# Products of the second expert table 512 columns wide, and a recurrent mixer worked in two halves

## Chip, core and metric

The kernel runs on one core of one Trainium2 chip. The metric is the device time of one execution in microseconds; the time before is the median of three runs. Engines are named as the profile names them: PE is TensorE's matmul, PEld its weight load, DVE is VectorE, ACT is ScalarE, POOL is GpSimd, and SP issues the transfers.

## What is computed

Two blocks of layers run over 256 tokens of width 1024. In the first block each of two layers has a mixer and an expert feed-forward network; the layers' modulation vectors come from `cond @ w_ada`. The change touches the feed-forward network's second table, in both layers, and the second layer's mixer.

```python
def peer_ffn(h, w_q, sub_keys, u_tab, v_tab):
    ...                                   # ids, gate: 16 experts of 16384 for each head and token
    def block(args):
        hx, idx, g = args
        u = u_tab[idx]
        act = jax.nn.gelu(jnp.einsum('thkd,td->thk', u, hx).astype(jnp.float32))
        return jnp.einsum('thk,thkd->td', g * act, v_tab[idx])

def rglru_mixer(h, w_in, conv_w, conv_b, w_a, b_a, w_x, b_x, lam, w_out):
    xb, yb = jnp.split(h @ w_in, 2, axis=-1)
    y_gate = jax.nn.gelu(yb)
    xc = sum(xp[:, j:j + S] * conv_w[j] for j in range(CONV_W)) + conv_b
    def direction(d, reverse):
        r = jax.nn.sigmoid(block_diag_linear(xc, w_a[d], b_a[d]))
        ig = jax.nn.sigmoid(block_diag_linear(xc, w_x[d], b_x[d]))
        log_a = -LRU_C * r * jax.nn.softplus(-lam[d])
        a = jnp.exp(log_a)
        mult = jnp.sqrt(-jnp.expm1(2.0 * log_a))
        return lax.associative_scan(lin_combine, (a, mult * ig * xc), axis=1, reverse=reverse)[1]
    return ((direction(0, False) + direction(1, True)) * y_gate) @ w_out
```

## The kernel before

Activations lie feature-major: 128 features on the partitions, the 256 tokens along a row, eight such tiles for the width of 1024. Every float32 operand of a large product is split in two, a rounded high part (a cast on ACT, line 283) and the low rest (a subtraction on DVE or POOL, line 285), and `mm3` (lines 412 to 418) makes one 128x128 weight tile into three matmuls: high by high, high by low, low by high. `Stream` cuts a matrix into blocks of 1024 columns (512 KB, eight weight tiles); `prefetch` takes a block from HBM into one of the four `raw` buffers and splits it into one of three `whi`/`wlo` pairs.

The expert network does not gather. `peer` multiplies all 16384 experts: 128 chunks of the first table (U), then 128 chunks of the second (V), 128 experts each. In the V part the weights of a matmul are a 128x128 tile of the table and its moving operand is the 128x256 tile of gated activations `A`; `product` runs `mm3` for the chunk's eight tiles, so a chunk is 24 matmuls of 256 columns. The outputs accumulate over all chunks, feature-major, in four PSUM banks. The last three chunks are done output by output, with `residual` behind each pair, and `lead.products` starts the next layer's first weights before the norm is known.

In layer 0 the V part also carries the next layer's modulation: `ada_sums` takes 48 blocks of `w_ada` through the same `raw` buffers, adds each into a row on DVE (lines 711 and 713), and after each eight sums over the partitions with four narrow matmuls (line 717).

`lru` is the mixer. The input branch (`lru_xb`: four outputs by `lead`, four by `linear`) goes through the convolution `evac` into `XC`; the gates (`lru_bd`) follow, 16 outputs of two kinds, with a step on DVE for each and a product on POOL; then the output gate (`lru_yb`, eight outputs in all four PSUM banks of `mm`), woven with `recurrences`, which goes by steps over both halves: all exponentials, all square roots, then four scans. The split of the product and `lru_out` come at the end.

A scheduler orders the instructions of each engine by a timeline of its own; `behind` and `pin` add an order written by hand. So the program's order and the engines' order can differ.

## Time and profile before

| | |
|---|---|
| median of three runs (lowest, highest) | 3035.58 us (3031.94, 3043.15) |
| profiled execution: its time | 3039.8 us |
| its span, first to last instruction | 3038.0 us |
| mean granted TensorE clock | 0.977 |
| V part of layer 0 | 759.9 to 1144.5 us of the span |
| mixer of layer 1, to the last matmul of `lead.products` | 1159.65 to 1303.4 us |
| V part of layer 1 | 1775.2 to 2147.0 us |

A matmul's end is modelled in this profile, and the records of consecutive matmuls overlap. How fast TensorE goes is therefore read from the distance between two starts, and not from the duration of one.

### The profile page before, as it was taken

To read this page: it belongs to the slowest core of one execution; us is meant where nothing else is said; L and a number is where in the kernel's file an instruction comes from. 1 tells how busy PE (TensorE), PEld (TensorE's weight loads), DVE (VectorE), ACT (ScalarE), POOL (GpSimd) and SP (SyncE) were. 2 spreads that over 40 slices of the span, in tenths; PEclk is the share of its full clock that TensorE was granted. 3 is DMA by queue.
4 is the path that set the end of the run, shared out by engine and by line. 5 is a ranking of instruction groups with operands and counts; after the bars stand their busy time and mean duration, and the time that the engine had idled before them with its cause. 6 is when DMAs were issued, how large, how long until landed. Compare 5 with 4: busy or idle time off the path is not lost. (4 is left out here: it accounts for less than half of the span.)

```text
span 3038.0 us, 58214 instructions
## 1 busy us (share of the span) xinstructions
PE 2868.7 (94%) x23408; PEld 2768.7 (91%) x23408; DVE 2249.4 (74%) x4115; ACT 1480.1 (49%) x2584; POOL 416.1 (14%) x260
## 2 busy tenths in 40 slices
PE   7999989999999998798999999999999989999898
PEld 7988989999999997698999999999888889977898
DVE  8997996887567659899788855555754688665885
ACT  3335434444444445554444444444744666455663
POOL 2232231000000004513200000000132020211201
PEclk9999999999999999899999999999999999999999
DMA  7655445555678763454555555665444346543454
GB/s 254 202 186 164 143 144 175 156 161 168 205 258 272 253 215 113 124 170 145 161 158 160 161 171 182 183 185 182 152 81 73 109 141 184 178 121 83 145 181 132
DMA packets 140143, 503.66 MB, mean 166 GB/s; under 512 B 15816, under 2 KB 18776, under 8 KB 139488
## 3 DMA queue, kind: packets, MB, share of 16 engines
q1 hardware_dynamic: 139872, 499.93, 53.7%
q8 instruction: 184, 3.01, 0.4%
q14 instruction: 87, 0.71, 0.1%
HBM read 496.72 MB, written 1.05 MB: 164 GB/s over the span
## 5 line engine op out<-in xcount | busy, mean ns | idle before, releaser
L415 PE MATMUL psmm<-xh,whi 128*128 128x256 f32 x5488 | 1568.2, 288 | 45.0 <-ACT xh L463 18.3
L417 PE MATMUL psmm<-xh,wlo 128*128 128x256 f32 x5488 | 1560.5, 286 | 40.4 <-DVE wlo L285 36.2
L416 PE MATMUL psmm<-xl,whi 128*128 128x256 f32 x5488 | 1565.7, 286 | 5.3 <-DVE xl L554 2.8
L283 ACT CAST whi<-raw 128x1024 fp32r<-128x1024 f32 x819 | 857.5, 1048 | 1231.6 <-PE psmm L416 924.7
L285 DVE TENSOR_TENSOR wlo<-raw,whi 128x1024 fp32r<-128x1024 f32 x740 | 939.7, 1272 | 452.0 <-ACT whi L283 445.7
L415 PEld LDWEIGHTS psmm<-xh,whi 128*128 128x128 f32 x5488 | 1058.6, 194 | 57.8 <-ACT xh L463 19.8
L417 PEld LDWEIGHTS psmm<-xh,wlo 128*128 128x128 f32 x5488 | 1062.2, 194 | 46.9 <-DVE wlo L285 41.8
L416 PEld LDWEIGHTS psmm<-xl,whi 128*128 128x128 f32 x5488 | 1065.0, 194 | 9.6 <-DVE xl L554 4.8
L285 POOL TENSOR_TENSOR wlo<-raw,whi 128x1024 fp32r<-128x1024 f32 x90 | 229.3, 2552 | 492.9 <-ACT whi L283 429.7
L285 POOL TENSOR_TENSOR Ar<-raw,Ar 128x1024 fp32r<-128x1024 f32 x4 | 9.6, 2402 | 1310.4 <-ACT Ar L283 1310.4
L415 PE MATMUL psst<-xh,whi 128*128 128x256 f32 x400 | 119.8, 301 | 0.0
L416 PE MATMUL psst<-xl,whi 128*128 128x256 f32 x400 | 118.9, 298 | 0.3 <-DVE xl L645 0.3
L417 PE MATMUL psst<-xh,wlo 128*128 128x256 f32 x400 | 118.0, 296 | 0.7 <-DVE wlo L285 0.7
L415 PE MATMUL psmm<-yh,whi 128*128 128x256 f32 x352 | 98.2, 280 | 0.0
L417 PE MATMUL psmm<-yh,wlo 128*128 128x256 f32 x352 | 97.9, 278 | 0.0
L416 PE MATMUL psmm<-yl,whi 128*128 128x256 f32 x352 | 97.5, 277 | 0.0
L713 DVE SCALAR_TENSOR_TENSOR oh<-raw,cond,oh 128x1024 f32<-128x1024 f32 x42 | 53.9, 1284 | 55.8 <-DMA raw<-in_ada 55.8
L1198 DVE TENSOR_TENSOR oh<-io,sel 128x512 f16<-128x512 f16 x128 | 54.2, 424 | 52.8 <-PE psac L1210 26.9
L464 DVE TENSOR_TENSOR xl<-A,xh 128x512 fp32r<-128x512 f32 x128 | 87.1, 684 | 0.0
L416 PEld LDWEIGHTS psst<-xl,whi 128*128 128x128 f32 x400 | 79.1, 198 | 7.2 <-issue 5.2
L415 PEld LDWEIGHTS psst<-xh,whi 128*128 128x128 f32 x400 | 79.0, 198 | 5.5 <-issue 4.5
L417 PEld LDWEIGHTS psst<-xh,wlo 128*128 128x128 f32 x400 | 79.2, 198 | 4.3 <-issue 2.8
(576 smaller groups left out, 3924.2 us busy)
## 6 DMA issues: line engine op xcount, KB each, us to landing
raw<-in_U SPq DMA_DIRECT2D x256, 512.0 KB, 3.6
raw<-in_V SPq DMA_DIRECT2D x256, 512.0 KB, 3.7
raw<-in_up SPq DMA_DIRECT2D x88, 512.0 KB, 3.7
raw<-in_ada SPq DMA_DIRECT2D x80, 512.0 KB, 4.4
raw<-in_down SPq DMA_DIRECT2D x44, 512.0 KB, 3.7
raw<-in_ev_in SPq DMA_DIRECT2D x42, 512.0 KB, 3.6
raw<-in_hg_in SPq DMA_DIRECT2D x40, 512.0 KB, 3.7
raw<-in_peer_q SPq DMA_DIRECT2D x32, 512.0 KB, 3.9
```

Of the source, the lines that this page charges most:

```text
L283: keep(nc.scalar.copy(hi, raw))
L285: keep(eng.tensor_tensor(lo, raw, hi.bitcast(F32), op=OP.subtract))
L415: first = t.matmul(ps, w[0], x[0], start=start, stop=False, **kw)
L416: t.matmul(ps, w[0], x[1], start=False, stop=False, **kw)
L417: t.matmul(ps, w[1], x[0], start=False, stop=stop, **kw)
L464: s.nc.vector.tensor_tensor(lo, src, hi.bitcast(F32), op=OP.subtract)
L713: nc.vector.scalar_tensor_tensor(acc, raw, s.cond[:, k:k + 1], acc, op0=OP.mult, op1=OP.add)
L1198: nc.vector.tensor_tensor(o1l, io4, k1, op=OP.is_equal)
```

## The change

**V part.** The operands change places. The 128x128 weights of a matmul are now a token half of a chunk's activations, and the table's rows are the moving operand, 512 columns in one matmul. A chunk is 12 matmuls (two halves of the features, two halves of the tokens, three products) into four whole PSUM banks, token-major. After the last chunk the four banks are copied to SBUF (`tok`), 16 transposes of 128x128 turn them feature-major in the two `ac` banks (`features`), and `residual` reads from there.

**Modulation.** `ada_sums` takes its blocks into four slots of `A`, the rows of the first 16 chunks, once these are used (`room`), and no longer into the `raw` buffers.

**Mixer.** The four input outputs that `lead` doesn't cover are computed tile by tile of the input in four banks; the evacuation of `lead`'s outputs is done in place in PSUM and put behind the norm. Four outputs of the gate branch come before the gates. Steps that went over one output go over four (`R_` by its constant, the tanh). POOL's products go to DVE, and most splits go from POOL to DVE with the casts on ACT. `recurrences` is called for one half at a time: the first runs beside the second half's gates, the second beside the last gate outputs and the first half of `lru_out`, which now accumulates tile by tile of its input.

The core of the diff:

```diff
-        u = s.ker.splp.tile([128, S], F32, name="sq", tag="sq", bufs=SQB)
+
+        u = ps[:, 0:S] if s.name == "lru_xb" else s.ker.splp.tile([128, S], F32, name="sq", tag="sq", bufs=SQB)
         w = s.ker.leadw[:, j, :]
         if s.n > S:
             nc.vector.tensor_copy(w, ps[:, S:S + 2])
         if m is None:
-            nc.vector.tensor_tensor(u, ps[:, 0:S], r, op=OP.mult)
+            ins = nc.vector.tensor_tensor(u, ps[:, 0:S], r, op=OP.mult)
+            if s.name == "lru_xb":
+                s.ker.behind(ins, s.ker.last_norm)
...
-                raw = s.raw_block(s.d[f"ada{layer}"][((r - 1 + layer) * KD + k) * 2 + e])
+                ap = s.d[f"ada{layer}"][((r - 1 + layer) * KD + k) * 2 + e]
+                if room:
+                    raw = room[k % len(room)]
+                    nc.sync.dma_start(raw, ap)
+                else:
+                    raw = s.raw_block(ap)
...
-            s.linear(s.stream("lru_xb"), x, KD, KD, evac, spare=XB_SP)
-            bd = s.stream("lru_bd", lo_pool=lambda b: b % BD_LO, hi_dve=lambda b: b % 4 < BD_HI)
+
+            w = s.stream("lru_xb")
+            ld, s.lead = s.lead, None
+            others = [bank()[:, :S] for bank in (s.mm, s.mm, s.stat, s.stat)]
+            for k in range(KD):
+                for ps in others:
+                    s.mm3(ps, next(w), (x[0][:, k, :], x[1][:, k, :]), k == 0, k == KD - 1)
+            for o in range(LEAD):
+                evac(o, ld.output(o, s.r, s.m))
+            for o, ps in enumerate(others):
+                evac(LEAD + o, ps)
+            yb = s.stream("lru_yb")
+            bd = s.stream("lru_bd", lo_pool=lambda b: b > 4 and b % 2)
...
-                            nc.scalar.activation(dst[:, o, :], ps, AF.Sigmoid, bias=s.v(b, d * KD + o))
-                        w = R_[d][:, o, :]
-                        nc.vector.tensor_scalar(w, w, cc[:, d * KD + o:d * KD + o + 1], None, op0=OP.mult)
-                    sl = slice(2 * n, 2 * n + 2)
-                    nc.gpsimd.tensor_tensor(IG[d][:, sl, :], IG[d][:, sl, :], XC[:, sl, :], op=OP.mult)
-                if n % 2:
-                    for d in range(2):
-                        hv = halves[n // 2]
-                        order.append(nc.scalar.activation(TH[d][:, hv, :], R_[d][:, hv, :], AF.Tanh, scale=0.5))
...
-            def recurrences():
-                for hv in halves:
-                    for d in range(2):
-                        a, ig = R_[d][:, hv, :], IG[d][:, hv, :]
-                        queue(nc.scalar.activation(a, a, AF.Exp, scale=-1.0))
-                        nc.vector.scalar_tensor_tensor(ig, a, 1.0, ig, op0=OP.add, op1=OP.mult)
...
-                for hv in halves:
-                    for d in range(2):
-                        a, ig, th, hs = (T[d][:, hv, :] for T in (R_, IG, TH, HS))
...
-                    nc.vector.tensor_tensor(HS[0][:, hv, :], HS[0][:, hv, :], HS[1][:, hv, :], op=OP.add)
+
+            hi, lo = s.acts()
...
+            def recurrences(h, gelus):
+
+                hv = slice(4 * h, 4 * h + 4)
+                for d in range(2):
+                    r = R_[d][:, hv, :]
+                    c = s.lru_cc[:, d * KD + 4 * h:d * KD + 4 * h + 4, None].to_broadcast([128, 4, S])
+                    nc.vector.tensor_tensor(r, r, c, op=OP.mult)
+                    queue(nc.scalar.activation(TH[d][:, hv, :], r, AF.Tanh, scale=0.5))
+                    queue(nc.scalar.activation(r, r, AF.Exp, scale=-1.0))
+                    nc.vector.tensor_tensor(IG[d][:, hv, :], IG[d][:, hv, :], XC[:, hv, :], op=OP.mult)
+                yield
+                for d in range(2):
+                    queue(nc.scalar.activation(TH[d][:, hv, :], TH[d][:, hv, :], AF.Sqrt))
+                    nc.vector.scalar_tensor_tensor(IG[d][:, hv, :], R_[d][:, hv, :], 1.0, IG[d][:, hv, :],
+                                                   op0=OP.add, op1=OP.mult)
+                yield
+                for first in gelus:
+                    gelu(first)
+                for d in range(2):
+                    a, ig, th, hs = (T[d][:, hv, :] for T in (R_, IG, TH, HS))
+                    nc.vector.tensor_tensor(ig, ig, th, op=OP.mult)
...
-            gate = gate_branch()
-            run_all(islice(gate, YL))
-            weave(gate, recurrences())
...
+                for j in (2 * h, 2 * h + 1):
+                    sl = slice(2 * j, 2 * j + 2)
+                    t = HS[0][:, sl, :]
+                    nc.vector.tensor_tensor(t, t, HS[1][:, sl, :], op=OP.add)
+                    nc.vector.tensor_tensor(t, t, YG[:, sl, :], op=OP.mult)
+                    s.split_into(hi[:, sl, :], lo[:, sl, :], t)
+                    yield
+
+            run_all(gate_branch((0, 1), s.ac), gate_branch((2, 3), s.ac))
+            for first in (0, 2):
+                gelu(first)
+            run_all(gates(0), gates(1))
+            weave(chain(gate_branch((4, 5), s.stat), gates(2), gates(3)), recurrences(0, ()))
...
+            pss = []
+
+            def product(k, o):
+                s.mm3(pss[o // 2][:, o % 2, :], next(out), (hi[:, k, :], lo[:, k, :]), k == 0 and o % 2 == 0,
+                      k == KD - 1, skip_group_check=True)
+
+            def first_half():
+                pss.extend(s.mm().rearrange("p (a b) -> p a b", a=2) for _ in range(4))
+                for k in range(4):
+                    for o in range(KD):
+                        product(k, o)
+                    yield
+
+            weave(chain(gate_branch((6, 7), s.ac), first_half()), recurrences(1, (4, 6)))
+            ev = s.residual(1, 0, lead)
+            for k in range(4, KD):
+                for o in range(4):
...
+                    for k in range(4, KD):
+                        product(k, o + e)
+                for f in after:
+                    f()
+                after = [ev(o + e, pss[o // 2][:, e, :]) for e in range(2)]
...
-            acc = [s.mm().rearrange("p (a b) -> p a b", a=2) for _ in range(4)]
-            vt = s.stream(f"V{layer}")
+
+            acc = [[s.mm() for _ in range(2)] for _ in range(2)]
+            vt = s.stream(f"V{layer}", width=WBLK)
...
+                return next(vt), (wh[:, c % 8, :], wl[:, c % 8, :])
+
+            def product(c, half, tt, v, w):
+
+                ts, fs = slice(tt * 128, (tt + 1) * 128), slice(half * 512, (half + 1) * 512)
+                for i, (a, b) in enumerate(((0, 0), (0, 1), (1, 0))):
+                    nc.tensor.matmul(acc[half][tt], w[a][:, ts], v[b][:, fs], start=c == 0 and i == 0,
+                                     stop=c == NK - 1 and i == 2)
...
+                room = [Af[:, n * WBLK:(n + 1) * WBLK] for n in range(RAW_A)]
+                row = oh.rearrange("p a b c -> p (a b c)").bitcast(F32)[:, 0:WBLK]
+                extra = chain(*(s.ada_sums(1, r, row, room) for r in range(3)))
...
-                if c % 2 and c > 8:
+                for half in range(2):
+                    for tt in range(2):
+                        product(c, half, tt, v, w)
+                if c % 2 and c >= 4 * RAW_A:
                     next(extra, None)
...
+            def features(half, tok):
+
+                for j in range(2):
+                    pt = s.ac().rearrange("p (a b) -> p a b", a=2)
+                    for e in range(2):
+                        for tt in range(2):
+                            nc.tensor.transpose(pt[:, e, tt * 128:(tt + 1) * 128],
+                                                tok[:, tt, (2 * j + e) * 128:(2 * j + e + 1) * 128], s.ident)
+                    yield [ev(4 * half + 2 * j + e, pt[:, e, :]) for e in range(2)]
+
+            toks = []
+            for half in range(2):
+                tok = s.rawp.tile([128, WBLK], F32, name="tok", tag="raw").rearrange("p (a b) -> p a b", a=2)
+                for tt in range(2):
+                    for c, v, w in last:
+                        product(c, half, tt, v, w)
+                    (nc.vector.tensor_copy if tt else nc.scalar.copy)(tok[:, tt, :], acc[half][tt])
+                toks.append(tok)
...
-            for j in range(KD // 2):
-                for o in (2 * j, 2 * j + 1):
-                    for c, v, w in last:
-                        product(c, o, v, w)
-                for f in after:
-                    f()
-                after = [ev(o, acc[j][:, o % 2, :]) for o in (2 * j, 2 * j + 1)]
+            for half, tok in enumerate(toks):
+                for fs in features(half, tok):
+                    for f in after:
+                        f()
+                    after = fs
```

On PE, at the end of layer 0's V part, before (`whi`, `wlo`: the split table; `xh`, `xl`: the split activations; `Ar`: the next layer's lead input; the numbers tell buffers apart):

```order
L415 MATMUL psmm_9028<-xh_9023,whi_13104 128x256
L416 MATMUL psmm_9028<-xl_9024,whi_13104 128x256
L417 MATMUL psmm_9028<-xh_9023,wlo_13105 128x256
L415 MATMUL psac_13253<-Ar_13109 128x258
L415 MATMUL psac_13254<-Ar_13109 128x258
L415 MATMUL psmm_13255<-Ar_13109 128x258
```

The same place now (`tok`: the copied banks; `cst`: the identity):

```order
L1325 MATMUL psmm_9027<-wlo_11557,xh_9023 128x512
L1325 MATMUL psmm_9027<-whi_11556,xl_9024 128x512
L1325 MATMUL psmm_9028<-wlo_11557,xh_9023 128x512
L1325 MATMUL psmm_9028<-whi_11556,xl_9024 128x512
L1361 MATMUL psac_11628<-cst_80,tok_11586 128x128
L1361 MATMUL psac_11643<-cst_80,tok_11586 128x128
L1361 MATMUL psac_11628<-cst_80,tok_11586 128x128 x3
L1361 MATMUL psac_11643<-cst_80,tok_11586 128x128 x3
L1361 MATMUL psac_11660<-cst_80,tok_11607 128x128 x4
L420 MATMUL psmm_11697<-Ar_11561 128x258
L420 MATMUL psmm_11698<-Ar_11561 128x258
L1361 MATMUL psac_11677<-cst_80,tok_11607 128x128 x4
```

A matmul of twice the width stands for two, and 16 transposes stand between the last product and nearly all of the next layer's first products. The scheduler works all four banks to the end together, where the program finishes one half first.

On DVE, in the middle of layer 0's V part, before (`oh` holds the modulation's row, `cond` its factor; one `wlo` is one chunk of the table):

```order
L713 SCALAR_TENSOR_TENSOR oh_3392<-raw_10650,cond_90,oh_3392 128x1024
L464 TENSOR_TENSOR xl_9024<-A_2917,xh_9023 128x512
L285 TENSOR_TENSOR wlo_10623<-raw_10620,whi_10622 128x1024
L285 TENSOR_TENSOR wlo_10658<-raw_10655,whi_10657 128x1024
L713 SCALAR_TENSOR_TENSOR oh_3392<-raw_10715,cond_90,oh_3392 128x1024
```

The same place now:

```order
L725 SCALAR_TENSOR_TENSOR oh_3392<-A_2917,cond_90,oh_3392 128x1024
L469 TENSOR_TENSOR xl_9024<-A_2917,xh_9023 128x512
L535 SCALAR_TENSOR_TENSOR gsc_88<-mod1_86,vecs_76 128x8
L287 TENSOR_TENSOR wlo_9579<-raw_9576,whi_9578 128x1024
L725 SCALAR_TENSOR_TENSOR oh_3392<-A_2917,cond_90,oh_3392 128x1024
L287 TENSOR_TENSOR wlo_9597<-raw_9594,whi_9596 128x1024
```

The sums stood one to two chunks; now they stand nearly one to one. Counted over the whole part, all 48 lie within 51 chunks, where before they were spread over 99.

On DVE, around the scans of the mixer, before (`HS` are the scans' outputs, `TH` the square roots, `R` and `IG` the gates, `YG` the gate branch):

```order
L1057 SCALAR_TENSOR_TENSOR HS0_13395<-R0_13397,IG0_13399 128x1024
L1054 TENSOR_TENSOR IG1_13400<-IG1_13400,TH1_13402 128x1024
L1060 SCALAR_TENSOR_TENSOR HS1_13396<-R1_13398,IG1_13400 128x1024
L1057 SCALAR_TENSOR_TENSOR HS0_13395<-R0_13397,IG0_13399 128x1024
L1060 SCALAR_TENSOR_TENSOR HS1_13396<-R1_13398,IG1_13400 128x1024
L1063 TENSOR_TENSOR HS0_13395<-HS0_13395,HS1_13396 128x1024 x2
L1073 TENSOR_TENSOR HS0_13395<-HS0_13395,YG_13394 128x512 x4
L464 TENSOR_TENSOR xl_14192<-HS0_13395,xh_14191 128x512 x4
```

The first half now, from its two scans on:

```order
L1084 SCALAR_TENSOR_TENSOR HS1_11838<-R1_11840,IG1_11842 128x1024
L1090 TENSOR_TENSOR HS0_11837<-HS0_11837,HS1_11838 128x512 x2
L1091 TENSOR_TENSOR HS0_11837<-HS0_11837,YG_11836 128x512 x2
L287 TENSOR_TENSOR wlo_12551<-raw_12548,whi_12550 128x1024
L1064 TENSOR_TENSOR R0_11839<-R0_11839,lru_cc_87 128x1024
L287 TENSOR_TENSOR wlo_12589<-raw_12586,whi_12588 128x1024
L1067 TENSOR_TENSOR IG0_11841<-IG0_11841,XC_11835 128x1024
L1064 TENSOR_TENSOR R1_11840<-R1_11840,lru_cc_87 128x1024
L1067 TENSOR_TENSOR IG1_11842<-IG1_11842,XC_11835 128x1024
L1071 SCALAR_TENSOR_TENSOR IG0_11841<-R0_11839,IG0_11841 128x1024
L1080 MEMSET R0_11839 128x4
L469 TENSOR_TENSOR xl_12024<-HS0_11837,xh_12023 128x512 x2
```

Two scans, where there were four, stand ahead of the first product with the gate branch, but the low part `xl` that `lru_out` waits for stands behind two splits and five steps of the second half.

## Rows read from the trace of the kernel before

**Rows 1.** The page's first part: busy time, share of the span, instructions.

```profile
PE 2868.7 (94%) x23408; PEld 2768.7 (91%) x23408; DVE 2249.4 (74%) x4115; ACT 1480.1 (49%) x2584; POOL 416.1 (14%) x260
```

**Rows 2.** Busy time by stretch, with granted clock, DMA share and GB/s.

```profile
core 0: us, PE busy (x) PEld busy (x) DVE busy (x) ACT busy (x) POOL busy (x), PEclk, DMA share, GB/s
759.90:1144.50 384.60, 378.37 (x3093) 371.12 (x3094) 251.10 (x252) 169.87 (x196) 3.44 (x2) 1.00 0.74 240
1775.20:2147.00 371.80, 369.65 (x3064) 369.04 (x3065) 197.69 (x197) 169.88 (x197) 4.53 (x2) 1.00 0.59 182
1159.65:1303.40 143.75, 107.94 (x776) 103.15 (x775) 125.14 (x151) 74.77 (x118) 73.28 (x32) 0.88 0.36 110
842.00:1092.00 250.00, 250.00 (x2059) 245.01 (x2057) 173.77 (x170) 110.48 (x129) 0.00 (x0) 1.00 0.81 263
5.00:30.00 25.00, 20.15 (x132) 17.08 (x132) 21.05 (x30) 7.97 (x15) 5.14 (x2) 1.00 1.02 409
```

**Rows 3.** Timeline of PE, V part of layer 1, then the 258-column products: start, duration.

```profile
1999.84 0.28 PE L417 MATMUL psmm<-xh,wlo 128*128 128x256 f32 x1
2000.68 0.28 PE L415 MATMUL psmm<-xh,whi 128*128 128x256 f32 x1
...
1297.07 0.28 PE L416 MATMUL psmm<-leadl,whi 128*128 128x258 f32 x1
1303.18 0.28 PE L416 MATMUL psmm<-leadl,whi 128*128 128x258 f32 x1
```

**Rows 4.** Line 928, plain float32 of 256 columns: durations, then timeline of eight.

```profile
L928 PE MATMUL psmm<-AT,V x32: 377/380/484, 223.1 to 236.5; 128*128 128x256 f32 x32
...
223.02 1.60 PEld L928 LDWEIGHTS psmm<-AT,V 128*128 128x128 f32 x8
223.13 1.89 PE L928 MATMUL psmm<-AT,V 128*128 128x256 f32 x8
```

**Rows 5.** Groups by line, V part of layer 0, 842 to 1092 us.

```profile
L285 DVE TENSOR_TENSOR wlo<-raw,whi 128x1024 fp32r<-128x1024 f32 x85 | 103.2, 1222 | 31.1 <-ACT whi L283 30.7
L283 ACT CAST whi<-raw 128x1024 fp32r<-128x1024 f32 x85 | 89.2, 1049 | 140.0 <-DMA raw<-in_V 65.5 <-PE psmm L416 59.1 <-PE psmm L417 6.0
L713 DVE SCALAR_TENSOR_TENSOR oh<-raw,cond,oh 128x1024 f32<-128x1024 f32 x35 | 44.9, 1284 | 36.1 <-DMA raw<-in_ada 36.1
L464 DVE TENSOR_TENSOR xl<-A,xh 128x512 fp32r<-128x512 f32 x42 | 28.7, 684 | 0.0
```

**Rows 6.** Timeline of PE in the mixer: three waits, with what ended them.

```profile
1199.08 0.49 PE L415 MATMUL psmm<-ch,whi 128*128 128x256 f32 x1 [3.85 <-ACT R L1017]
1217.28 0.58 PE L415 MATMUL psmm<-xh,whi 128*128 128x256 f32 x1 [4.81 <-ACT R L1017]
1263.18 1.23 PE L415 MATMUL psmm<-xh,whi 128*128 128x256 f32 x4 [14.64 <-ACT xh L463]
```

**Rows 7.** Timeline of DVE in the mixer: start, duration, count.

```profile
1159.94 0.88 DVE L550 SCALAR_TENSOR_TENSOR sq<-xres,gsc,sqacc 128x256 f32<-128x256 f32 x2
1167.06 0.42 DVE L333 TENSOR_TENSOR sq<-psac,sqacc 128x256 f32<-128x256 f32 x1
1167.47 0.48 DVE L554 SCALAR_TENSOR_TENSOR xl<-sq,mod,xh 128x256 fp32r<-128x256 f32 x1
1169.02 2.19 DVE L993 SCALAR_TENSOR_TENSOR XC<-sq,vecs,XC 128x254 f32<-128x254 f32 x5
1228.30 4.56 DVE L1043 SCALAR_TENSOR_TENSOR IG<-R,IG 128x1024 f32<-128x1024 f32 x2
1234.54 1.21 DVE L1054 TENSOR_TENSOR IG<-IG,TH 128x1024 f32<-128x1024 f32 x1
1255.27 4.36 DVE L1060 TENSOR_TENSOR_SCAN HS<-R,IG 128x1024 f32<-128x1024 f32 x1
1264.21 2.48 DVE L464 TENSOR_TENSOR xl<-HS,xh 128x512 fp32r<-128x512 f32 x4
```

**Rows 8.** Groups by line on POOL, mixer, 1159.6 to 1300 us.

```profile
L285 POOL TENSOR_TENSOR wlo<-raw,whi 128x1024 fp32r<-128x1024 f32 x19 | 55.9, 2953 | 41.7 <-DVE whi L281 24.5 <-issue 7.2 <-ACT whi L283 5.4
```

**Rows 9.** Timeline of PE at the end of layer 1's V part, the last product's wait.

```profile
2143.19 0.39 PE L417 MATMUL psmm<-xh,wlo 128*128 128x256 f32 x1 [1.39 <-DVE wlo L285]
```

More of the change, by code (lines that the diff above doesn't have):

```diff
@@ L112 @@
 OUT_LO = 3
-YB_LO, BD_LO, XB_SP, BD_HI, LY, YL, YB_HI = 8, 4, 2, 9, 1, 4, (3, 4, 5)
 HELD_O, DIFF = 2, 3
@@ L117, with tiles_of @@
 NST = 4
+RAW_A = 4
 PL = 1, 3
 ADDED, ADDED_LN = 6, 4
-def tiles_of(w, lead=LEAD):
+def tiles_of(w, lead=LEAD, groups=1):
     K, N = w.shape
     t = w.reshape(K // 128, 128, N // 128, 128)
-    first = t[:, :, :lead].transpose(0, 2, 1, 3).reshape(-1, 128, 128)
-    return np.concatenate([first, t[:, :, lead:].transpose(2, 0, 1, 3).reshape(-1, 128, 128)], 0)
+    first = [t[:, :, g * lead:(g + 1) * lead].transpose(0, 2, 1, 3).reshape(-1, 128, 128) for g in range(groups)]
+    return np.concatenate([*first, t[:, :, groups * lead:].transpose(2, 0, 1, 3).reshape(-1, 128, 128)], 0)
 def blocks(t):
@@ L701, in first_norm, with ada_sums @@
         return hi, lo
-    def ada_sums(s, layer, r, acc):
+    def ada_sums(s, layer, r, acc, room=()):
         nc = s.nc
@@ L1077, in lru @@
+            after = [ev(o, pss[o // 2][:, o % 2, :]) for o in range(4)]
+            for o in range(4, KD, 2):
+                for e in range(2):
[6 more added lines that the diff above has]
+                f()
             lead.products()
```

85 lines of the change are left out of this document (36 added, 49 removed).

## The prediction

> **What bounds the kernel now.** The page's first part comes first: PE is busy for 94% of the span [rows 1]. Busy is not yet a bound, so the stretches come next. In both V parts PE is busy nearly throughout at a granted clock of 1.00, while DVE works 251 of 385 us and 198 of 372 us; in the mixer PE does 108 of 144 us at a clock of 0.88 and DVE 125 [rows 2]. So the V parts hang on PE's pace, the mixer on a chain through DVE, and each part of the change has to be priced in its own stretch.
>
> The third view is the timeline, for the pace. In layer 1's V part seven matmuls start within 0.84 us, 120 ns apart [rows 3]. A layer is 128 x 24 = 3072 of them, 368.6 us; the stretch took 371.8, so 3.2 us are its start and end. Layer 0's took 384.6: the other 12.8 are the modulation's sums on PE and waits for split blocks.
>
> What sets the 120 ns decides the case. Two rows bear on it. The 258-column products of the same kind make 51 starts in 6.11 us, 119.8 ns apart [rows 3]: two more columns should have cost 0.94 ns each time if the columns set the pace, and they cost nothing. And plain float32 of 256 columns, with a new 128x128 weight tile each time, starts every (1.89 - 0.38) / 7 = 216 ns [rows 4]. That is about twice 107, as if its columns went through twice; the weight loads don't add to it. I read from both that 256 columns need some 107 ns, that the remaining 13 are a floor of each matmul with its load, and that a longer pass covers the floor.
>
> **The V parts.** A chunk falls from 24 matmuls to 12 with the same columns in all. The trace has no split float32 matmul of 512 columns. From below its pace is 216 ns, line 928's [rows 4]; from above 2 x 119.8 = 239.6, if time goes by columns after all [rows 3]; between them lies 216 + 13 = 229, if the floor is paid with every matmul whatever its length. I take 216, since line 928 also streams long, changes its weights each time and shows nothing above it. A layer's products are then 1536 x 0.216 = 331.8 us instead of 368.6: 36.8 less.
>
> *What is late next.* Per chunk ACT has a cast of 1.05 us and half a cast of activations, DVE 1.22 + 0.34 = 1.56 us [rows 5], against 2.59 for PE. In layer 1 nothing else comes near. Transfers rise to 0.524 MB in 2.59 us, 202 GB/s.
>
> *The end of the part* gets longer. The order finishes all four banks together, so the copies wait for the last products; then come eight transposes, the residual's steps on DVE out of two banks, eight transposes more, and only then the next layer's products in `ac`. By the residual's chain (a copy of some 0.7 us, two rounds of four DVE steps of 0.45, the transposes' 1.8 us on PE) I put 5 us between the last product and a running `lead.products`, where a single wait of 1.4 us stood near the end before [rows 9], so 3 us more. Layer 1: 331.8 + 3.2 + 3 = 338.0, a gain of 33.8 us.
>
> *Layer 0 and the modulation.* The new buffers take its blocks out of the ring of `raw`, so the 65.5 us in which ACT waited for the table and the 36.1 in which DVE waited for `w_ada` [rows 5] lose that cause. But the order now has 48 sums in 51 chunks. There DVE needs 1.56 + 48/51 x 1.284 = 2.77 us by single durations [rows 5], some 2.6 with the overlap of consecutive steps, so it is level with PE's 2.59. The transfers need 99 blocks, 51.9 MB, in 51 x 2.59 = 132 us: 393 GB/s. The kernel's start, with many buffers open, ran at 409; the same V part at 263 [rows 2]. At 409 nothing is lost; at 263 the 51 chunks take 197 us, 65 more. I take 15: both sides now have four buffers of their own, which is nearer to the start's case than to four shared ones, but DVE, PE and transfers all stand at their limit together. PE's own sums lie under that. Layer 0: 331.8 + 6.2 + 15 = 353.0, a gain of 31.6 us.
>
> The Trainium skill's page "DMA: Bandwidth & Descriptors" (Specifications) gives about 358 GB/s as what HBM yields to one core; by it, an estimate, the 51 chunks would take 145 us, 13 more than PE needs. The start's 409 GB/s is above that figure, so this trace doesn't bear the limit out for a core alone; the 15 would stand about there anyway.
>
> **The mixer.** The matmuls are the same, 672 from the input branch on and 96 of `lead.products`: 92 us at 120 ns, of 143.75 [rows 2]. The largest wait is 14.64 us for the split of the product, behind four scans; two of 3.85 and 4.81 stand at the gates [rows 6]. I lay the new DVE order on the old durations, from the same zero at 1159.65:
> - the norm's 16 steps, as before to 1167.9 [rows 7], one split: 1169. Eight steps of 0.38 on `lead`'s outputs and two splits of 1.2: 1174.5. PE has the other four outputs meanwhile.
> - 24 convolution steps of 0.44 (five in 2.19 [rows 7]), four splits of 0.62, one block: 1188.8. The first gate-branch outputs need the two `ac` banks, which the convolution frees at about 1181.5, a new wait of PE. Then 96 matmuls to 1193, and 96 for the first two gate blocks to 1205.
> - first half: eight steps or splits of 1.17, two scans of 4.4, four steps of 0.62: 1226. Two splits and five steps of the second half come ahead of `xl`: 8.2 + 1.2, so 1235.6. PE has 17 us of gates and outputs until about 1230 and waits 5.
> - second half: three steps, two scans, three splits, six short steps: 1255. PE's first half of `lru_out` (11.5 us) ends at 1247 and waits 8. The other 96 matmuls end at 1266.5, `lead.products` 12 us later, at 1278.5.
>
> Before it was 1303.4: 25 us less. One cost is uncertain, POOL. With POOL at work two wide DVE steps took 4.56 us, where one alone took 1.21 [rows 7]; POOL had 19 splits of 2.95 us there [rows 8] and keeps five (two of the gates, three of `lru_out`), so about 15 us of POOL work stay, and up to half of that may come back on DVE. From above: all 22 wide steps slowed by 1.07 would eat 24 us, the whole gain; from below: nothing slowed, and the banks free earlier, 28. I take 20, near the lower count of POOL's work.
>
> **Sum.** 33.8 + 31.6 + 20 = 85 us from the profiled execution's 3039.8: 2954. That execution lies 4 us above the median of the three, so 2950 against 3035.6.
>
> **Rivals.**
> 1. *The transfers hold layer 0.* The dense stretch goes at the 263 GB/s of before: 50 us more, 3000. For it: ACT's 65.5 us for the table's blocks. Against: those buffers were shared.
> 2. *The floor is paid in full,* 229 ns: 3072 x 13 ns, less 8 us hidden in the dense stretch, 32 us more: 2982. For it: nothing in the trace has this operand form at this length. Against: line 928.
> 3. *Columns set the pace,* 239.6 ns: 72.5 us more, 15 of them hidden: 3008. Against: the 258-column rows.
> 4. *The mixer gains nothing,* DVE slowed throughout by POOL: 2970.
> 5. *Slower: the weight loads lie bare.* If a load can't run under a 512-column pass, the 120 ns come on top: 336 ns, 3072 x 120 ns = 369 us more, 3319. It decides from 85 / 3072 = 28 ns a matmul on, a pace of 244. Against it: line 928's loads run between its starts and its pace holds no room for them.
>
> The Trainium skill's page "TensorE: Matmul & The Clock Gate" (Part 3, The mechanism) states a rule that speaks for the fifth: a weight load overlaps matmuls in flight only where the row groups differ, and here both use all rows. By that rule line 928 would have to be slower than its columns; this trace disagrees, at 216 ns.
>
> **How the numbers follow.** My forecast has 0.60 (its own range 2930 to 2975), the rivals 0.12, 0.10, 0.07, 0.05 and 0.03; 0.03 is left for mixtures. The range of 2928 to 2998 takes in forecast, second and fourth rival and most of the first: low is a layer 0 with nothing lost (15 us) and a mixer at 27. About 0.5%, or 15 us, is what a measurement tells from no change: slower has the fifth rival's 0.03, same 0.04 from a third rival with a poor mixer, faster 0.93.
>
> **What would show it.** Right: starts 216 ns apart in layer 1's V part and a stretch near 338 us; in layer 0 a slower middle where the sums are, and 2.59 us a chunk behind it; in the mixer waits of 5 to 8 us where 14.64 stood, and the end about 119 us behind its start. Wrong: starts at 229 or more; ACT or DVE waiting for transfers for tens of us in layer 0; DVE steps of over 2 us throughout the mixer.

## The result, and the profile after

The changed kernel takes 2985.75 us (median; 2984.50 to 2989.92) against 3039.36 us for the kernel before on the same chips: a ratio of 0.9822, 95% interval 0.9807 to 0.9838. It is faster by 54 us, where 85 were forecast. The time lies in the stated range of 2928 to 2998, but outside the forecast's own of 2930 to 2975 and 36 us above its centre: the range holds it because it was drawn to take in the second rival. It is that rival's time (2982), and as the runs below show, largely by that rival's mechanism.

The page of the changed kernel, first part (busy time, share of the span, instructions), answers to [rows 1]:

```profile
PE 2833.1 (95%) x20368; PEld 2616.1 (88%) x20368; DVE 2240.5 (75%) x4113; ACT 1499.2 (50%) x2603; POOL 364.2 (12%) x241
```

PE is still busy for 95% of the span, with 3040 fewer matmuls. As before, that share says nothing about where the time went; the stretches do. Both profiled executions are cut at the same landmarks on PE, each at the start of a matmul (so the ends differ by 1 or 2 us from those of [rows 2]); rows are rounded one by one:

| stretch, us | before | after | change |
|---|---|---|---|
| start to the first V product of layer 0 | 759.9 | 759.6 | -0.3 |
| V part of layer 0, first to last product | 386.4 | 358.2 | -28.2 |
| its end: to the first product behind the next norm | 14.7 | 18.8 | +4.1 |
| mixer: to the last matmul of `lead.products` | 142.3 | 126.0 | -16.3 |
| the norm behind it: to the next part's first transposes | 7.6 | 13.9 | +6.3 |
| U part of layer 1 | 464.4 | 464.1 | -0.3 |
| V part of layer 1 | 372.7 | 349.7 | -23.0 |
| its end | 14.4 | 19.6 | +5.2 |
| everything behind (code that the change doesn't touch) | 875.7 | 873.2 | -2.5 |
| span | 3038.0 | 2983.1 | -54.9 |

So layer 0's V part with its end gave 24.1 us, layer 1's 17.8 and the mixer with the norm behind it 9.9. Forecast were 31.6, 33.8 and 20.

Busy time by stretch after, with granted clock, DMA share and GB/s, as in [rows 2]: the V part of layer 0, of layer 1, two pieces of layer 0's in which the modulation's sums stand, and the mixer.

```profile
759.60:1118.05 358.45, 357.64 (x1572) 289.62 (x1572) 252.91 (x250) 171.29 (x198) 3.88 (x2) 1.00 0.75 256
1740.65:2090.55 349.90, 349.90 (x1536) 289.48 (x1536) 202.20 (x194) 168.94 (x193) 2.85 (x2) 1.00 0.60 190
795.00:845.00 50.00, 50.00 (x222) 39.50 (x221) 47.54 (x49) 22.78 (x26) 0.00 (x0) 1.00 1.00 377
795.00:920.00 125.00, 125.00 (x548) 97.50 (x547) 113.59 (x112) 57.03 (x67) 0.00 (x0) 1.00 0.94 349
1134.25:1262.90 128.65, 103.16 (x771) 101.49 (x770) 105.53 (x139) 87.73 (x130) 25.88 (x13) 0.89 0.36 116
```

In layer 1's V part PE has 1536 matmuls and no idle time at all, at a clock of 1.00: what it takes is its pace. In layer 0's dense stretch the transfers ran at 377 GB/s for 50 us, and PE was busy for all 50.

Timeline of PE, layer 1's V part after, answering to [rows 3] (start, duration):

```profile
2080.58 0.39 PE L1325 MATMUL psmm<-wlo,xh 128*128 128x512 f32 x1
...
2083.30 0.39 PE L1325 MATMUL psmm<-wlo,xh 128*128 128x512 f32 x1
```

Twelve matmuls start in these 2.72 us, 226.7 ns apart. The forecast had 216 and the second rival 229. Over 1536 matmuls that is 348.2 us of the 349.7.

Timeline of PE in the mixer and behind it after, answering to [rows 6]: the waits of over 2 us, with what ended them.

```profile
1156.59 0.55 PE L420 MATMUL psac<-xh,whi 128*128 128x256 f32 x1 [6.68 <-DVE XC L1004]
1198.21 0.58 PE L420 MATMUL psmm<-ch,whi 128*128 128x256 f32 x1 [7.00 <-ACT R L1053]
1219.00 1.03 PE L420 MATMUL psmm<-xh,whi 128*128 128x256 f32 x4 [4.38 <-ACT xh L468]
1222.20 0.58 PE L421 MATMUL psmm<-xl,whi 128*128 128x256 f32 x1 [2.17 <-DVE xl L469]
...
1238.36 0.39 PE L420 MATMUL psmm<-xh,whi 128*128 128x256 f32 x1 [2.54 <-ACT whi L285]
...
1268.07 0.58 PE L420 MATMUL psmm<-xh,whi 128*128 128x256 f32 x1 [3.88 <-ACT xh L556]
```

The 14.64 us of before are gone; six smaller waits stand there, and the last of them is behind the mixer, where before PE went on with `lead.products` until the norm was done.

### The profile page after: what moved, and what is told of

The parts are those of the page before. It is cut to its first block, busy times and chain, and to the rows that moved or that the text cites. A ratio compares the mean times of both kernels' runs of the same rounds, so it can differ in the third digit from the quotient of the medians.

```text
span 2983.1 us, 52247 instructions
## 1 busy us (share of the span) xinstructions
PE 2833.1 (95%) x20368; PEld 2616.1 (88%) x20368; DVE 2240.5 (75%) x4113; ACT 1499.2 (50%) x2603; POOL 364.2 (12%) x241
## 5 line engine op out<-in xcount | busy, mean ns | idle before, releaser
L420 PE MATMUL psmm<-xh,whi 128*128 128x256 f32 x3376 | 968.8, 290 | 28.6 <-ACT whi L285 8.6
L422 PE MATMUL psmm<-xh,wlo 128*128 128x256 f32 x3376 | 959.3, 286 | 28.1 <-DVE wlo L287 28.1
L421 PE MATMUL psmm<-xl,whi 128*128 128x256 f32 x3376 | 963.1, 286 | 2.9 <-DVE xl L469 2.2
L420 PEld LDWEIGHTS psmm<-xh,whi 128*128 128x128 f32 x3376 | 651.7, 195 | 35.2 <-ACT whi L285 10.8
L422 PEld LDWEIGHTS psmm<-xh,wlo 128*128 128x128 f32 x3376 | 654.2, 194 | 32.1 <-DVE wlo L287 32.0
L421 PEld LDWEIGHTS psmm<-xl,whi 128*128 128x128 f32 x3376 | 657.0, 195 | 4.2 <-DVE xl L469 2.5
L1325 PE MATMUL psmm<-wlo,xh 128*128 128x512 f32 x1024 | 400.1, 391 | 0.8 <-DVE wlo L287 0.8
L1325 PE MATMUL psmm<-whi,xl 128*128 128x512 f32 x1024 | 397.9, 390 | 0.0
L1325 PE MATMUL psmm<-whi,xh 128*128 128x512 f32 x1024 | 277.9, 390 | 3.6 <-ACT xh L468 3.6
L1325 PEld LDWEIGHTS psmm<-whi,xl 128*128 128x128 f32 x1024 | 192.8, 188 | 40.0
```

The costliest lines, as they stand in the source:

```text
L420: first = t.matmul(ps, w[0], x[0], start=start, stop=False, **kw)
L421: t.matmul(ps, w[0], x[1], start=False, stop=False, **kw)
L422: t.matmul(ps, w[1], x[0], start=False, stop=stop, **kw)
L1325: nc.tensor.matmul(acc[half][tt], w[a][:, ts], v[b][:, fs], start=c == 0 and i == 0, stop=c == NK - 1 and i == 2)
```

## The experiments

All are read by the stretches of the table, because the totals carry something else: the part behind layer 1's V part, whose code no experiment edits, took between 868 and 887 us. What was seen of that stands under e9.

**One part of the change at a time: e1 and e2.** e1 is the changed kernel with the mixer of before:

```diff
-            run_all(gate_branch((0, 1), s.ac), gate_branch((2, 3), s.ac))
...
-            weave(chain(gate_branch((6, 7), s.ac), first_half()), recurrences(1, (4, 6)))
...
+            s.linear(s.stream("lru_xb"), x, KD, KD, evac, spare=XB_SP)
...
+            s.linear(s.stream("lru_out", lo_pool=lambda b: b < OUT_LO), (hi, lo), KD, KD, s.residual(1, 0, lead))
```

> The changed kernel with the mixer of before: only the second table's products 512 wide and the modulation's blocks in used rows remain. Theory (a fixed part of 13 ns in every split matmul beside its columns): starts 226.6 ns apart, V parts of 358 and 350 us, the tails 2 and 4 us longer, so 42 us less than before: about 2997. Rival (the mixer's 9 to 10 us in the traces are a shift and nothing stays of them): the whole 53 us come from here, about 2986.

Measured: 3010.00 us against 3037.45, ratio 0.9915 (0.9886 to 0.9943). By stretches the theory holds: both V parts with their ends are 24.1 and 17.6 us shorter, 41.7 in all, and the mixer is as before (150.4 us with its norm against 149.8). The total missed by 13 us, since 7.2 were lost behind layer 1 (882.9 us) and 3.1 ahead of layer 0. The rival is out: nothing near 53 us comes from the V parts.

e2 is the changed kernel with the V parts and the modulation of before:

```diff
-            acc = [[s.mm() for _ in range(2)] for _ in range(2)]
-            vt = s.stream(f"V{layer}", width=WBLK)
...
+            acc = [s.mm().rearrange("p (a b) -> p a b", a=2) for _ in range(4)]
+            vt = s.stream(f"V{layer}")
```

> The kernel before with the mixer in halves alone. Theory (the mixer's end comes 15 us earlier, but 6 us of that are lost again at the norm behind it): 9 to 11 us less than before, about 3029. Rival (the 20 us of the prediction, the rest hidden by the V part's change): about 3019. Other rival (nothing): 3039.

Measured: 3032.60 against 3037.45, ratio 0.9986 (0.9975 to 0.9998). The mixer ends 13.6 us earlier and the next part's transposes start 7.9 us earlier. So the mixer alone is worth 5 to 8 us, less than the 9 to 11 expected and not 20, with the V parts of before as well; the gain was not hidden by the rest of the change.

**Width or exchange of operands: e3.**

```diff
-                    nc.tensor.matmul(acc[half][tt], w[a][:, ts], v[b][:, fs], start=c == 0 and i == 0,
...
+                    for q in range(0, 512, 256):
+                        nc.tensor.matmul(acc[half][tt][:, q:q + 256], w[a][:, ts], v[b][:, half * 512 + q:half * 512 + q + 256],
```

> The changed kernel with each 512-column product cut into two of 256, operands still exchanged. Theory (a fixed part per matmul): starts 120 ns apart, 240 for what takes 226.6, so 1536 x 13.4 = 20.6 us more per layer, 41 in all: about 3027. Rival (the exchange of the operands brings the gain, not the width): unchanged, about 2986.

Measured: 3024.99 us, 39 more than the changed kernel (ratio to before 0.9963, 0.9949 to 0.9977). Busy time by stretch, the V part of layer 1 with halved width:

```profile
1760.10:2128.70 368.60, 368.58 (x3071) 368.58 (x3072) 202.25 (x194) 169.50 (x195) 4.19 (x2) 1.00 0.59 182
```

3072 matmuls in 368.6 us are 120.0 ns each again, so width is what gives 18.9 us here, and the exchange of operands by itself nothing: this V part with its end (368.6 + 18.4) takes what it took before (372.7 + 14.4). That every matmul carries a fixed part of about 13 ns stands.

**What the pace depends on: e5.** In layer 1's V part the 512 columns are cut into two unequal pieces, 14 chunks for each pair:

```diff
+        return ((384, 128), (320, 192), (448, 64), (258, 254), (272, 240), (256, 256), (480, 32))[i]
...
+                    for w_ in s.widths(layer, c):
+                        nc.tensor.matmul(acc[half][tt][:, q:q + w_], w[a][:, ts], v[b][:, half * 512 + q:half * 512 + q + w_],
```

> The changed kernel; in layer 1's V part 98 of the 128 chunks cut each 512 columns into two pieces, 14 chunks for each pair: 384+128, 320+192, 448+64, 258+254, 272+240, 256+256, 480+32. Read is the distance between starts by width. Theory (a line through 256 columns at 120 ns and 512 at 226.6): 13.3 ns + columns x 0.4167, so 213.3 for 480, 200 for 448, 173.3 for 384, 146.7 for 320, 126.7 for 272, 120.8 for 258, 113.3 for 240, 93.3 for 192, 66.7 for 128, 40 for 64 and 26.7 for 32; 98 x 12 x 13.3 ns = 15.7 us more in this part. Rival 1 (the prediction's reading of the 258-column rows: a floor that a longer pass covers): all from 258 down to 240 lie at 120, and 272 to 384 at columns x 0.4167 = 113 to 160, below the line. Rival 2 (the weight load sets a least time of its own): the line holds from some width on and is flat below it.

Measured in one execution: this part took 403.3 us, 53.6 more than in the changed kernel, where 15.7 were expected. Busy time of e5 in the stretches of 384+128, 448+64, 258+254 and 256+256, each from the first to the last start of a wide piece (167 pairs; 335 matmuls in the last):

```profile
1754.38:1802.19 47.81, 47.81 (x335) 47.81 (x334) 22.01 (x21) 18.31 (x21) 0.00 (x0) 1.00 0.47 155
1845.96:1898.24 52.28, 52.28 (x337) 49.94 (x335) 22.01 (x21) 18.27 (x21) 0.00 (x0) 1.00 0.43 142
1898.55:1938.71 40.16, 40.16 (x337) 40.16 (x336) 22.01 (x21) 18.23 (x21) 0.00 (x0) 1.00 0.55 183
1978.60:2018.80 40.20, 40.20 (x337) 40.20 (x336) 22.01 (x21) 18.29 (x21) 0.00 (x0) 1.00 0.56 183
```

A pair takes 286.3, 313.0, 240.5 and 240.0 ns; by the same reading 480+32 takes 330.6, 320+192 258.8 and 272+240 236.1. The pair 258+254 lies on the theory's line (240.0), but its columns add up to 512 like those of 256+256, so a floor common to both widths would give the same: this pair tests nothing. The pairs with a narrow piece lie off the line. From 320+192 over 384+128 to 448+64 a pair grows by 54.2 ns for 128 columns more in the wide piece, 0.42 ns each, and the columns that the narrow piece loses save nothing. Take the line's 13.3 ns + columns x 0.4167 off for the wide piece, and the narrow one costs 117 ns at 32 columns, 113 at 64, 113 at 128, 112 at 192 and 109 at 240 (the line would have 113.3 there, so that pair lies 4 ns under it). The first rival is out by 512 columns alone, which would take 213.3 ns by it. So there are two regimes, as in the second rival of the experiment: a matmul with a weight load of its own takes 13.3 ns + columns x 0.4167, but, beside a wider one, not less than about 113 ns. By this reading 256 columns stand only 7 ns above that least time, and 512 pay the fixed 13.3 ns once instead of twice. Two things are not shown. Only the sum of a pair is measured: the single starts divide it otherwise (in one pair of 480+32 the wide piece starts at 2046.65 us, the narrow one at 2046.95 and the next wide one at 2046.98). And that the weight load sets the least time is the rival's reason; every piece has a load of its own, and no run leaves the loads out.

The Trainium skill's page "TensorE: Matmul & The Clock Gate" (Part 3, The mechanism) says that a weight load overlaps matmuls in flight only where the row groups differ, but also that a load into the background weight buffer is pulled ahead. Here all rows are used, a load's record lasts 188 ns on average, and 213.3 of the 226.7 ns are the columns' own time, so a load is covered in the main. These runs disagree with the first sentence, as line 928 did by the forecast's reading [rows 4], and agree with the second.

**The modulation's blocks in the shared ring: e4.**

```diff
-                extra = chain(*(s.ada_sums(1, r, row, room) for r in range(3)))
+                extra = chain(*(s.ada_sums(1, r, row) for r in range(3)))
```

> The changed kernel with the modulation's blocks through the ring of raw buffers, as before. The order then spreads the 48 sums over 99 chunks again. Theory (layer 0 keeps the single waits of 1 us of before, five of them, and nothing else): 3 to 8 us more than the changed kernel, about 2991. Rival (shared buffers hold the transfers at 263 GB/s): 99 chunks with 147 blocks, 77.1 MB, take 293 us where the products take 269, so 24 us more: 3010. Other rival (the slots bring nothing): 2986.

Measured: 3014.72 us, 29 more than the changed kernel; 13 of them lie behind layer 1 (886.6 us). Layer 0's V part takes 374.9 us, 16.7 more, between theory and rival. Its stretch, and the waits in it (total, times, longest):

```profile
759.35:1134.30 374.95, 362.43 (x1572) 289.95 (x1572) 248.88 (x250) 174.50 (x196) 3.29 (x2) 1.00 0.74 245
```

```profile
DVE oh L725 <- DMA raw<-in_ada: 80.4, 42, 3.6
...
ACT whi L285 <- DMA raw<-in_V: 61.4, 56, 2.6
```

Here DVE and ACT wait for transfers that run at 245 GB/s on average, though the sums are spread over 99 chunks. With four buffers of their own, the same blocks came at 349 GB/s over 125 us (795 to 920); in that time ACT waited for them once, for 2.7 us, and DVE not at all. It is the buffers, then, that set the rate, and the slots in `A` are worth 16.7 us at the new pace.

**The mixer's end: e6 and e7.** In the changed kernel POOL works splits between the sums of squares that the next norm waits for. Timelines of POOL, of DVE and of ACT after, from the last outputs of the mixer on:

```profile
1250.26 2.42 POOL L287 TENSOR_TENSOR wlo<-raw,whi 128x1024 fp32r<-128x1024 f32 x1 [0.43 <-ACT whi L285]
1252.64 0.92 POOL L497 TENSOR_TENSOR sqacc<-sqacc,sq 128x256 f32<-128x256 f32 x1
1253.52 2.59 POOL L287 TENSOR_TENSOR wlo<-raw,whi 128x1024 fp32r<-128x1024 f32 x1
1256.07 0.92 POOL L497 TENSOR_TENSOR sqacc<-sqacc,sq 128x256 f32<-128x256 f32 x1
1256.96 2.58 POOL L287 TENSOR_TENSOR wlo<-raw,whi 128x1024 fp32r<-128x1024 f32 x1
1259.50 0.92 POOL L497 TENSOR_TENSOR sqacc<-sqacc,sq 128x256 f32<-128x256 f32 x1
```

```profile
1254.16 5.66 DVE L317 SCALAR_TENSOR_TENSOR leadl<-xres,gsc,leadh 128x256 fp32r<-128x256 f32 x3
...
1265.14 1.75 DVE L508 RECIPROCAL sqacc<-sqacc 128x256 f32<-128x256 f32 x1
```

```profile
1260.95 0.41 ACT L491 ACTIVATE sq<-xres 128x256 f32<-128x256 f32 x1
```

POOL's last addition of squares ends at 1260.4 and ACT's last square at 1261.4. PE takes up their sum over the partitions only behind `lead.products`, at 1262.74, and the norm's reciprocal starts 2.4 us behind the last matmul of `lead.products` (1262.7). In the kernel before it started ahead of it, at 1296.46 where those products ran until 1303.3:

```profile
1296.46 1.75 DVE L503 RECIPROCAL sqacc<-sqacc 128x256 f32<-128x256 f32 x1 [1.54 <-ACT sqacc L502]
```

e6 takes these three splits from POOL:

```diff
-        s.ahead = Stream(s, follow, lo_pool=lambda b: (b in PL) if store else 0 < b < 4, store=store)
+        s.ahead = Stream(s, follow, lo_pool=lambda b: (b in PL) if store else 0 < b < 4 and follow != "peer_q1", store=store)
```

> The changed kernel with the three splits on POOL for the next layer part's first weights, which stand among the sums of squares at the mixer's end, moved to DVE. Theory (POOL's splits hold up the norm's sums and slow DVE): from the last product of the mixer to the first transposes behind the norm 9 to 10 us instead of 13.9, so 4 to 5 us less in all, about 2981. Rival (the eight outputs come too close together for ACT and DVE, whoever makes the splits): 13 to 15 us, about 2986.

Measured: the norm behind the mixer takes 9.3 us instead of 13.9, as the theory had it; the total is 2994.97, 9 us above the changed kernel, since 887.0 us stand behind layer 1. Timelines of POOL and DVE in e6: the squares are summed without a break, and the reciprocal starts before `lead.products` end at 1262.1.

```profile
1248.87 3.69 POOL L497 TENSOR_TENSOR sqacc<-sqacc,sq 128x256 f32<-128x256 f32 x3 [0.80 <-ACT sq L491]
```

```profile
1258.37 1.75 DVE L508 RECIPROCAL sqacc<-sqacc 128x256 f32<-128x256 f32 x1
```

e7 leaves POOL and finishes the outputs one after the other (the weights are laid out accordingly):

```diff
-            for k in range(4, KD):
-                for o in range(4):
-                    product(k, o)
-            after = [ev(o, pss[o // 2][:, o % 2, :]) for o in range(4)]
-            for o in range(4, KD, 2):
+            after = []
+            for o in range(0, KD, 2):
```

> The changed kernel with the second half of the mixer's last product worked one output after the other, where four outputs ran together and then four one by one. Theory of e6 (POOL): the same 13.9 us behind the last lead product, 2986. Rival (bunched outputs): the first outputs are ready 4.3 us earlier, so the residual and the norm end 3 to 4 us earlier, about 2982.

Measured: mixer and norm 136.9 us, 3.0 less than 139.9, so the rival has a share too; the total is unchanged at 2986.48, with 4.4 us lost ahead of layer 0's V part and 2.6 at its end. The 6.3 us behind the mixer have both causes: POOL's three splits, 4.6 us, and the outputs' coming close together, 3.0 us; as these add up to more than 6.3, they overlap.

**POOL in the second half's gates: e8.**

```diff
-            bd = s.stream("lru_bd", lo_pool=lambda b: b > 4 and b % 2)
+            bd = s.stream("lru_bd")
...
-            out = s.stream("lru_out", lo_pool=lambda b: b < OUT_LO)
+            out = s.stream("lru_out")
```

> The changed kernel with none of the gates' and of the last product's splits on POOL (five fewer there, five more of 1.2 us on DVE). Theory (the three splits of POOL at 1212 to 1221.6 us of the span slow the DVE steps beside them, 2.81 and 2.71 us where 1.2 and 0.7 are usual, and PE waits 4.65 and 2.59 us there): the mixer 3 to 4 us shorter, about 2982. Rival (DVE's own added work of 6 us takes the place): unchanged or up to 3 us longer, 2986 to 2989.

Measured: the mixer 121.3 us to the end of `lead.products` (126.0) and 133.9 with the norm (139.9), 4.7 and 6.0 less. The total is 2990.82, with 886.3 us behind layer 1. DVE at the place in question, first the changed kernel, then e8:

```profile
1216.58 2.81 DVE L1071 SCALAR_TENSOR_TENSOR IG<-R,IG 128x1024 f32<-128x1024 f32 x1 [2.81 <-ACT R L1066]
1219.43 2.71 DVE L469 TENSOR_TENSOR xl<-HS,xh 128x512 fp32r<-128x512 f32 x1
```

```profile
1218.77 1.23 DVE L1071 SCALAR_TENSOR_TENSOR IG<-R,IG 128x1024 f32<-128x1024 f32 x1 [1.14 <-ACT R L1066]
...
1221.80 1.29 DVE L469 TENSOR_TENSOR xl<-HS,xh 128x512 fp32r<-128x512 f32 x2
```

POOL in the changed kernel at that place:

```profile
1212.00 6.30 POOL L287 TENSOR_TENSOR wlo<-raw,whi 128x1024 fp32r<-128x1024 f32 x2 [9.73 <-ACT whi L285]
1218.50 3.09 POOL L287 TENSOR_TENSOR wlo<-raw,whi 128x1024 fp32r<-128x1024 f32 x1 [0.20 <-ACT whi L285]
```

Beside these splits the two steps took 2.81 and 2.71 us; without them 1.23 and 0.65. The splits ended 1.7 and 2.2 us behind the steps' starts, and by 1.6 and 2.1 us the steps were longer. Five splits more on DVE cost less than they gave back. The Trainium skill's page "SBUF — State Buffer" (Who interferes with whom) says that a VectorE instruction with two inputs in SBUF contends with a GpSimd instruction that reads SBUF, and that their shared pair of ports is an exclusive lock; the rows agree, as each step was longer by about the rest of a split.

**The part that nothing edits: e9.** The edits of e7 and e8 together.

> The changed kernel with the edits of e7 and e8 together. In this one the order behind the second expert layer comes out nearly as in the changed kernel, in e8 it did not. Theory (the stretch behind layer 1's V part is longer only where that order differs): this stretch 872 to 876 us as in e7, where e8 had 886; the mixer to the transposes behind its norm 3 + 6 = 9 us shorter than 139.9; in all about 2977. Rival (splits moved to DVE make the later part longer): stretch of 884 to 887, about 2988.

Measured: 2984.75 us. The part behind layer 1 took 879.2 us, between theory and rival, and the mixer with its norm 135.6 instead of the 131 expected, so the two edits overlap. In all runs the later part has the same 6272 matmuls, and two things go with its length. Where ACT has 28 to 30 loads of its function tables there (e1, e4, e6, e8), it takes 883 to 887 us; where it has 24 or 25 (all others), 868 to 879. And within the second group the granted clock differs, as the first 100 us of that part show in e7 (872.7 us in all) and then in e9 (879.2):

```profile
2111.80:2211.80 100.00, 95.06 (x656) 82.42 (x656) 66.39 (x168) 60.40 (x129) 17.99 (x35) 0.97 0.35 98
```

```profile
2105.20:2205.20 100.00, 96.96 (x621) 84.16 (x622) 64.38 (x167) 57.39 (x123) 16.71 (x34) 0.88 0.30 97
```

That the edits shift how the scheduler orders that code is plain from the table loads; what in an edit shifts it was not isolated and stays open. For reading the experiments it means that a total can't tell effects smaller than this part's range of 19 us, and a stretch can.

**Versions that might be better: e10 and e11.** e10 has the edits of e6, e7 and e8, and puts the second half's last V products behind the first half's:

```diff
+                    if first is not None:
+                        s.behind(ins, first)
```

> The edits of e6, e7 and e8 together, and in both V parts the second half's last products put behind the first half's, so that the first two banks are copied and turned while the other two are finished. Theory: the copies' wait goes off the path, 2 to 3 us less at the end of each V part; the mixer to the transposes behind its norm 10 to 12 us shorter than 139.9; the later stretch 873 to 876: about 2968. Rival (the end of a V part hangs on the second half's own copies, transposes and residual, so half of the wait stays; and the three edits of the mixer take the same wait away twice): 1 us per layer and 7 us in the mixer, about 2976.

Measured: 2977.26 us, ratio 0.9788 (0.9771 to 0.9805), but not by the theory. Layer 0's V part became 5.2 us longer, because the first half's products now reach the last chunks before these are split (PE waited 1.85 us for `wlo` at 1118.03, and from 1118.9 to 1121.9 the granted clock was 0.50), its end stayed at 19.5 us, and the mixer with its norm took 138.7. The gain came from the U part of layer 1 (453.8 us, where all others have 463 to 466) and the part behind (867.9). Why the U part is shorter there was not followed up.

e11 has the edits of e6 and e8 alone.

> The edits of e6 and e8 together, with the end of the V parts as in the changed kernel. Theory (POOL's splits cost at two places of the mixer, in the second half's gates and at the norm behind it, one after the other on the chain): the mixer to the transposes behind its norm 4.5 + 6.0 = 10.5 us shorter, 129.4 us. Rival (the two edits take the same wait away): 133 to 135 us. The stretch behind layer 1's V part, with the same 6272 matmuls, has taken 873 to 887 us; if TensorE's granted clock there accounts for the difference it is 873 to 876 at a mean clock of 0.96 or more over its first 100 us and 880 or more at 0.88 or less; so in all 2973 to 2985.

Measured: 2975.82 us, ratio 0.9787 (0.9770 to 0.9803), the best of all: 63 us below the kernel before. The mixer with its norm takes 130.6 us, 9.3 less than in the changed kernel where 10.5 were expected, so the two waits on POOL lie one behind the other and both are real. The part behind is 871.9 us at a clock of 0.95 over its first 100 us, where 873 to 876 were expected from 0.96 on.

## Why the prediction was right and where it was wrong

**The bound** was read rightly: the V parts hang on PE's pace at a full clock, the mixer on a chain. The V parts gave 41.9 of the 54.9 us, the mixer 9.9.

**The pace** is the step that failed: 216 ns taken, 226.7 measured. The forecast's 36.8 us per layer become 20.4, 3072 x 120.0 ns less 1536 x 226.7; that is 16.4 us per layer and 33 in both, more than the 30 us by which the whole gain fell short. The rival had it: 13 ns paid with every matmul whatever its length. Two readings led away from it. Line 928 was taken as the nearest row because it is long and changes its weights, but it is another kind of matmul, plain float32, and its 2.7 ns above the columns' time (if they go through twice, as the forecast read it) are not the split kind's 13.3. And the 258-column rows were used to say that two more columns cost nothing: a slope was read from two points 2 columns, or 0.8 ns, apart. In e5 the pair 258+254 takes 240.5 ns, which line and floor alike would give. Those rows themselves (119.8 ns before, and in the changed kernel 95 steps of `lead.products` in 11.41 us, 120.1) still lie a little under the line's 120.8; that rest stays open. What e5 shows of a floor lies at about 113 ns and under 256 columns, and 512 columns don't cover the 13.3 ns but pay them too.

**The end of the V parts** was rightly seen as a cost and put at 3 us; it is 4.1 and 5.2. PE's wait for the copies has a part that the forecast didn't name. ACT loads the table for the coming square root in front of its copies:

```profile
2090.04 1.28 ACT L513 ACT_TABLE_LOAD   x1
...
2091.44 1.05 ACT L1371 COPY tok<-psmm 128x512 f32<-128x512 f32 x2
```

**Layer 0's dense stretch** was put at 15 us, and the first rival at 50 more; it cost about 1. Layer 0's V part takes 10.0 us above its products' 348.2, and layer 1's 1.5; of the difference of 8.5, 7.5 lie at the nine places where the sums' own narrow matmuls stand between the products. The mistake is in a row that is in plain view: 263 GB/s was taken for what shared buffers yield, but in that stretch PE was busy for 250.00 of 250.00 us [rows 2]. It was what the kernel asked for, and no limit. The limit of shared buffers is near there all the same, as e4 shows, so the slots are needed, for a reason that the row could not carry. Above its products the layer took 10.0 us where 18.2 were forecast (3.2 and 15), so this term gave back 8 us of what the pace lost.

**The mixer** was laid out to end 25 us earlier, less 5 for POOL. It ended 16.3 us earlier, and 6.3 of these were lost again behind it. The first wait, for the `ac` banks, was forecast from 1174.5 to 1181.5, 14.9 to 21.9 us behind the zero (the end of the `lead.products` ahead, 1159.65 before and 1134.25 after); it ended at 22.3, after a wait of 6.7 us. The 5 us for POOL were the right size (e8: 4.7). What failed is that only DVE and PE were laid out. ACT's queue holds tanh, exponential and square root of the first half ahead of the next gates' sigmoids, with a table load of 1.28 us at each change, and PE waited 7.00 us for a sigmoid to free a bank; `lru_out` started at 84.8 us behind the zero, where 76 were laid out. Timeline of ACT after, ahead of that sigmoid:

```profile
1194.36 2.00 ACT L1070 ACTIVATE TH<-TH 128x1024 f32<-128x1024 f32 x2
1196.38 1.28 ACT L1053 ACT_TABLE_LOAD   x1
1197.68 0.47 ACT L1053 ACTIVATE R<-psmm,vecs 128x256 f32<-128x256 f32 x1
```

And the end was set at the last matmul of `lead.products`, as if the norm behind were hidden there as before. Its squares are now ready so late (e6, e7) that PE adds them up only behind these products; what this order on PE adds by itself was not isolated.

**The other rivals** are out: columns don't set the pace alone (239.6 ns), the weight loads don't lie bare, and DVE was slowed by POOL at two places and not throughout.

**The signs that were named** told it apart: starts at 229 or more were to show the forecast wrong, and 226.7 came; there were no waits for transfers of tens of us in layer 0; and the mixer's end stood 128.6 us behind its start, not 119.

## What to carry to other kernels

Read a fixed cost per instruction from rows of the same kind at lengths that differ by much, or leave both slope and floor open; a row of another data type is not the nearest row, however alike its shape. A measured rate is a limit only where somebody waited for it; ask first whether the consumer was busy all the time. And where a chain is shortened, lay out every engine's queue, and follow it to the next point at which the engine that sets the time would have waited anyway: here that was the norm behind the mixer, and more than a third of what the mixer gained stayed there.

## What the hardware showed that was not expected

- Split float32 matmuls with a weight load each: 120.0 ns at 256 columns and 226.7 at 512, so 13.3 ns + columns x 0.4167 ns, and beside a wider one not less than about 113 ns if a pair's time is divided as under e5. At a granted clock of 0.50, the lower of the two levels (1741.8 to 1744.8 us of the changed kernel), those of 512 columns start 427 ns apart, 0.833 ns a column and nothing above it: there the 13.3 ns don't show. The Trainium skill's page "TensorE: Matmul & The Clock Gate" (Part 2, What happens when you issue a matmul) gives 512 / 2.4 + some 2.5 ns, 216, as the distance of two matmuls; for this kind 226.7 was measured.
- One core alone drew 377 GB/s from HBM over 50 us beside a PE that was busy throughout.
- Three splits on POOL at the mixer's end and five in its middle cost 4.6 and 6.0 us net of the work that they took from DVE (e6, e8), and nearly the sum of both was won by taking all of them away (e11: 9.3).
